# Two MLPs in float32 on one core: w1 in products of 256 columns, its parts laid at other byte offsets per group

## The chip, the core and the metric

One NeuronCore of a Trainium2 chip runs the whole program. The metric is the device time of one execution in microseconds (us). The kernel before takes 2183.7 us, the median of two runs (2183.35 and 2184.06). The execution that was profiled took 2184.25 us. A measurement of this kernel is taken to tell a difference of 2%, which is 43.7 us here.

## The reference, cut to what matters

The model has two layers over 256 tokens of width 2048: stick-breaking attention, an MLP, native sparse attention, and a second MLP. What the change touches is the first half of both MLPs (2048 to 8192 columns) and some projections of the attentions:

```python
def sqrelu_mlp(h, w1, w2):
    return jnp.square(jax.nn.relu(h @ w1)) @ w2

# stick_breaking_attention
q, k, v = jnp.split(h @ w_qkv, 3, axis=-1)
# native_sparse_attention
q, kc, vc, ks, vs, kw, vw, gl = jnp.split(h @ w_in, offs, axis=-1)
```

All arrays are float32, and the result has to be as good as float32. TensorE is used in float32r, which rounds its operands. So each operand is kept as two parts, hi (the rounded value) and lo (what the rounding left), and a product x·w becomes three: xhi·whi, xlo·whi and xhi·wlo.

## The kernel before

The program is one stream of products on TensorE (PE), written out in the order in which it runs. Weights come from HBM in pieces of 512 KB (`load`, L139, on the queue of SP, into five buffers `raw`). ScalarE (ACT) rounds a piece to `hi` (L134), VectorE (DVE) subtracts to get `lo` (L136). `hi` and `lo` have four buffers each.

- **Tile offsets.** `split` (L130) makes its two tiles 64 elements (256 bytes) longer than a piece, and the argument `o` says at which element the piece begins in each: NEAR is 0 bytes, FAR 64 bytes, LOW 208 bytes and SUM 192 bytes. A tile is 4352 bytes long, which is a whole number of 256 bytes, so all four buffers begin at the same remainder modulo 256 bytes. In the built program `xs`, `yhi`, `ylo`, `ss` and the tiles of `hi` and `lo` all begin at that same remainder. So `o`, in bytes, is also the distance modulo 256 between what a product loads as weights and what it streams. This is called the **place** below.
- **proj_T2 (L195)**, used by the first half of the MLPs. `hi` is the stationary operand (the weights in the array), and `xs` holds xhi and xlo side by side, so that one product of 512 columns (L203) makes hi·xhi and hi·xlo at once, into the two halves of one PSUM bank. A second product, of 256 columns (L210), adds lo·xhi to the first half. A piece of 128 by 128 of w1 costs one of each. They run in runs of 16 and 16: two pieces of w1, then the next two. `hi` lies at place 0 and `lo` at place 208.
- **group1 (L440)**. The 8192 columns are done in four groups per MLP (`fg`), each in four blocks of 512 columns (`fb`), so there are 32 blocks in the program. A block has 64 pieces of 128 by 128, and uses four banks of one PSUM pool, `acc` and `att` by turns. At its end ACT copies the second halves (L449, four times), DVE adds the first ones (L450, four times), and one DVE instruction does the relu and the scale by row (L451).
- **proj_T2h (L216)** is the same for 256 columns of weights at a time: four rows of blocks by two, runs of 8 products of 512 columns (L224) and 8 of 256 (L230). It makes q and k of head groups 1 to 3 and the two inputs of the compression: 16 calls of four chunks. `evac_T2` (L237) joins its halves.
- **chunk_T (L178)** serves the first head group alone, at the start of the program. It is the older form: three products of 256 columns for each piece (L185), hi·xhi, hi·xlo and lo·xhi, 16 with `hi` and then 8 with `lo`, both at place 64.
- **The first chunk** is made by `chunk_first` (L547): the same products of 256 columns (L550), with tiles at place 0.
- **group2 (L468)** multiplies by w2. There the weights of the array are `yhi`, `ylo` and `ss`, and w2 streams: products of 512 columns (L156) and, for a quarter of the columns, 21 products of 256 columns per piece (L280, `chunk_S`). w2's parts stream from place 192 there, so that the stationary operand lies 64 bytes past them modulo 256.

Work of the attention and of the next stage is recorded between the products by `pump` (L106), which is called twice per piece.

Of the kernel before, what the change touches and what calls it, by code (L numbers as in the profile page):

```python
# [25 lines left out]
KC = 2  # L26
# [13 lines left out]
def hybrid_kernel(  # L40
# [65 lines left out]
    def pump():  # L106
        if beside:
            b = beside[0]
            b[2] += b[1] / KC
            while b[2] >= 1:  # L110
                b[2] -= 1
                y = next(b[0], b)
                if y is b:
                    beside.remove(b)
                if y:
                    break
# [6 lines left out]

    PAD = 64
    NEAR, FAR, LOW, SUM = 0, 16, 52, 48

    def split(raw, o=(NEAR, NEAR)):  # L130
        n = KC * NB
# [14 lines left out]
    def load_split(*where, o=(NEAR, NEAR)):  # L146
        return split(load(*where), o)

    def bank(pool, tag):
        return pool.tile([P, NB], F32, tag=tag, name=tag)  # L150
# [24 lines left out]
                mm(ahi, lo[:, kk, :], k, t, False, last and kk == KC - 1)  # L175
            pump()

    def chunk_T(ps, src, k0, n0, first, last):  # L178

        hi, lo = src if isinstance(src, tuple) else load_split(src, k0, KC, n0, NB, o=(FAR, FAR))  # L180
        tiles = [(kk, m) for kk in range(KC) for m in range(NB // P)]

        def mm(w, x, kk, m, s, e):
            o = ps[m // 2][:, (m % 2) * T:(m % 2 + 1) * T]
            nc.tensor.matmul(o, w[:, kk, m * P:(m + 1) * P], x[:, k0 + kk, :], start=s, stop=e, skip_group_check=True)  # L185

        for kk, m in tiles:
            mm(hi, xhi, kk, m, first and kk == 0 and m % 2 == 0, False)
            mm(hi, xlo, kk, m, False, False)
        pump()  # L190
        for kk, m in tiles:
            mm(lo, xhi, kk, m, False, last and kk == KC - 1)
        pump()

    def proj_T2(ps, src, n0):  # L195


        for k0 in range(0, KD, 2 * KC):
            parts = [load_split(src, k0 + i * KC, KC, n0, NB, o=(NEAR, LOW)) for i in range(2)]
            tiles = [(k0 + i * KC + kk, m, *(a[:, kk, m * P:(m + 1) * P] for a in parts[i]))  # L200
                     for i in range(2) for kk in range(KC) for m in range(NB // P)]
            for j, (k, m, hi, lo) in enumerate(tiles):
                nc.tensor.matmul(  # L203
                    ps[m], hi, xs[:, k, :, :].rearrange("p a t -> p (a t)"), start=k == 0, stop=k == KD - 1,
                    skip_group_check=True,
                )
                if j % 8 == 7:
                    pump()
            for j, (k, m, hi, lo) in enumerate(tiles):
                nc.tensor.matmul(  # L210
                    ps[m][:, :T], lo, xhi[:, k, :], start=False, stop=k == KD - 1, skip_group_check=True,
                )
                if j % 8 == 7:
                    pump()

    def proj_T2h(src, n0):  # L216

        ps = [bank(acc, "acc") for _ in range(2)]
        KH, W = 2 * KC, NB // 2
        for k0 in range(0, KD, KH):  # L220
            hi, lo = load_split(src, k0, KH, n0, W, o=(NEAR, LOW))
            tiles = [(kk, m) for kk in range(KH) for m in range(2)]
            for kk, m in tiles:
                nc.tensor.matmul(  # L224
                    ps[m], hi[:, kk, m * P:(m + 1) * P], xs[:, k0 + kk, :, :].rearrange("p a t -> p (a t)"),
                    start=k0 + kk == 0, stop=k0 + kk == KD - 1, skip_group_check=True,
                )
            pump()
            for kk, m in tiles:
                nc.tensor.matmul(  # L230
                    ps[m][:, :T], lo[:, kk, m * P:(m + 1) * P], xhi[:, k0 + kk, :],
                    start=False, stop=k0 + kk == KD - 1, skip_group_check=True,
                )
            pump()
        return ps

    def evac_T2(dst, ps, row):  # L237

        c = small.tile([P, 2, T], F32, tag="part", name="part", bufs=1)
        for j in range(2):  # L240
            nc.scalar.activation(c[:, j, :], ps[j][:, T:], AF.Copy)
            nc.vector.tensor_tensor(dst[:, j, :], ps[j][:, :T], c[:, j, :], op=OP.add)
        nc.vector.tensor_tensor(dst, dst, row.unsqueeze(1).to_broadcast([P, 2, T]), op=OP.mult)

    def chunk_S(ps, src, k0, n0, first, last, ahi, alo, shi, slo, koff=0):

# [67 lines left out]
    def proj_N(src, n0, pool=acc, tag="acc"):  # L314
        ps = [bank(pool, tag) for _ in range(NT)]
        for k0 in range(0, KD, KC):
            chunk_N(ps, src, k0, n0, k0 == 0, k0 + KC == KD, xhi, xlo)
        return ps

    def proj_T(src, n0):  # L320
        ps = [bank(acc, "acc") for _ in range(2)]
        for k0 in range(0, KD, KC):
            chunk_T(ps, src, k0, n0, k0 == 0, k0 + KC == KD)
        return ps

    def split_evac(hi, lo, src, scale=None):
# [103 lines left out]
    def mlp(l, layer, junk, done, last=None):  # L430
# [9 lines left out]
        def group1(fg, pools):  # L440

            for fb in range(D // NB):
                ps = [bank(*pools[fb % 2]) for _ in range(NB // P)]
                proj_T2(ps, w1, fg * D + fb * NB)
                k, n = fb * (NB // P), NB // P
                a = junk.tile([P, n, T], F32, tag="pre", name="pre", bufs=1)
                for j in range(n):
                    c = junk.tile([P, T], F32, tag="part", name="part")
                    nc.scalar.activation(c, ps[j][:, T:], AF.Copy)  # L449
                    nc.vector.tensor_tensor(a[:, j, :], ps[j][:, :T], c, op=OP.add)  # L450
                nc.vector.scalar_tensor_tensor(  # L451
                    a, a, 0.0, row.unsqueeze(1).to_broadcast([P, n, T]), op0=OP.max, op1=OP.mult
                )
                s = junk.tile([P, n, T], F32, tag="sq", name="sq", bufs=1)
                nc.scalar.activation(s, a, AF.Square)
                nc.scalar.activation(yhi[:, k:k + n, :], s, AF.Copy)
                nc.vector.tensor_tensor(ylo[:, k:k + n, :], s, yhi[:, k:k + n, :].bitcast(F32), op=OP.subtract)

                sv = s.rearrange("p (j kk) t -> p j kk t", kk=2)
                a1, a2 = [[sv[:, :, kk, t * P:(t + 1) * P] for kk in (1, 0)] for t in range(NT)]  # L460
                q = junk.tile([P, 2, 4, P], F32, tag="sums", name="sums", bufs=1)
                nc.vector.scalar_tensor_tensor(q[:, :, 0, :], a2[0], -1.0, a2[1], op0=OP.mult, op1=OP.subtract)
                nc.vector.tensor_tensor(q[:, :, 2, :], a1[0], a2[0], op=OP.subtract)
                nc.vector.tensor_tensor(q[:, :, 1, :], a2[1], q[:, :, 2, :], op=OP.subtract)
                nc.vector.tensor_tensor(q[:, :, 3, :], a1[1], q[:, :, 1, :], op=OP.subtract)
                split_evac(ss[:, 0, k // 2:k // 2 + 2], ss[:, 1, k // 2:k // 2 + 2], q)
# [44 lines left out]
    with tc.tile_pool(name="sbp", bufs=2) as sp:  # L511
# [171 lines left out]
        for hg in range(NH // HG):  # L683
            qT = sp.tile([P, HG, T], F32, name="qT")
            kT = sp.tile([P, HG, T], F32, name="kT")
            v = sp.tile([P, NT, NB], F32, name="v")
            if hg == 0:
                spawn(first_factors(qT, kT), 1)
            else:
                for b in range(2):  # L690
                    evac_T2(qT[:, 2 * b:2 * b + 2, :], proj_T2h(sb_w_qkv[0], hg * NB + b * T), rows[:, 0, :])
                for b in range(2):
                    evac_T2(kT[:, 2 * b:2 * b + 2, :], proj_T2h(sb_w_qkv[0], D + hg * NB + b * T), rows[:, 1, :])
            psv = proj_N(sb_w_qkv[0], 2 * D + hg * NB, *((att, "att") if hg == 0 else ()))
            for t in range(NT):
                nc.scalar.activation(v[:, t, :], psv[t], AF.Copy, scale=factor[0][:, t:t + 1])

            drain()
            spawn(attention(hg, qT, kT, v), 0.6 if hg < NH // HG - 1 else 1.1)
# [20 lines left out]
    with tc.tile_pool(name="nsa", bufs=2) as ap, ExitStack() as last:  # L720
# [255 lines left out]
        for i in range(2):  # L976
            cT = cp.tile([P, G, T], F32, tag="cT", name="cT", bufs=1)
            for b in range(2):
                ps = proj_T2h(w_in, C0 + i * NB + b * T)
                if rstd is None:  # L980
                    rstd = make_rstd("nsa")
                    pb = bcast_rows(rstd)
                    rb = cp.tile([P, T], F32, name="rb2", bufs=1)
                    nc.scalar.activation(rb, pb[:, :T], AF.Copy)
                evac_T2(cT[:, 2 * b:2 * b + 2, :], ps, rb)
            spawn(compress(i, cT), 1.8)


# [117 lines left out]
```

## Time and profile before

| | |
|---|---|
| median of the runs | 2183.7 us |
| the profiled execution | 2184.25 us |
| its span, first to last instruction | 2182.2 us |
| PE busy | 2172.6 us, 11922 products and as many weight loads |
| DVE busy | 1524.8 us |
| ACT busy | 1210.8 us |
| granted TensorE clock over the span | 1.000 of full speed |

The profile shows a product from its issue to its end, and products overlap. So the time that one product costs is read from the start of one run of products to the start of the next, divided by their number, and not from the duration of one. A row of the view in order of time holds a run of like instructions: its start, the time from the first start to the last end, the engine, line, operation, what it writes and reads, the sizes and the count.

### The profile page before, as it was taken

How to read it: one execution, taken by the hardware profiler on the slowest of the kernel's cores; microseconds unless marked ns; L12 is line 12 of the kernel's file. 1: busy time of each engine (PE TensorE's matmuls, PEld its weight loads, DVE VectorE, ACT ScalarE, POOL GpSimd, SP SyncE). 2: the span in 40 equal slices, each digit the busy share in tenths (PEclk: the TensorE clock that was granted, in tenths of full speed). 3: DMA queues.
4: the chain of work that ended last, by engine and by line, in shares of the span. 5: the costliest groups of instructions: out<-in, count | busy, mean ns of one | idle time of the engine just before them, and what ended most of it. 6: DMA issues, size and time to landing. Idle time of an engine off the chain costs nothing.

```text
span 2182.2 us, 31326 instructions
## 1 busy us (share of the span) xinstructions
PE 2172.6 (100%) x11922; PEld 1880.7 (86%) x11922; DVE 1524.8 (70%) x2096; ACT 1210.8 (55%) x1697; POOL 42.5 (2%) x75
## 2 busy tenths in 40 slices
PE   9999999999999999999999999999999999999999
PEld 9888888888888888888888888888888888888888
DVE  5656656677677677668777877755777676777685
ACT  5555665555455465456555666655554554654553
POOL 0000000000000000000000011000000000000000
PEclk9999999999999999999999999999999999999999
DMA  7655555565665665665667554456656656656664
GB/s 232 206 172 174 157 182 176 181 186 191 205 191 181 216 190 180 217 192 185 206 181 219 160 145 140 137 165 184 188 181 212 193 174 213 193 180 210 191 198 157
DMA packets 260766, 405.97 MB, mean 186 GB/s; under 512 B 13188, under 2 KB 91912, under 8 KB 260616
## 3 DMA queue, kind: packets, MB, share of 16 engines
q1 hardware_dynamic: 259800, 403.52, 59.6%
q8 instruction: 93, 1.52, 0.3%
q10 hardware_dynamic: 816, 0.46, 0.1%
q14 instruction: 57, 0.47, 0.1%
HBM read 401.83 MB, written 2.10 MB: 185 GB/s over the span
## 4 chain that ended last, share of the span: by engine, by line
PE 99%; DVE 0%; POOL 0%; ACT 0%; issue 0%; DVEq 0%; ACTq 0%; POOLq 0%
PE acc L156 31%; PE att L156 13%; PE acc L203 11%; PE att L203 11%; PE acc L210 5%; PE att L210 5%; PE acc L224 5%; PE att L280 4%; PE acc L280 4%; PE acc L230 3%; PE acc L185 2%; PE att L938 1%; PE att L343 1%; PE att L930 0%; PE att L931 0%; PE att L932 0%
## 5 line engine op out<-in xcount | busy, mean ns | idle before, releaser
L136 DVE TENSOR_TENSOR lo<-raw,hi 128x1024 fp32r<-128x1024 f32 x687 | 830.9, 1220 | 386.4 <-issue 170.0
L134 ACT ACTIVATE hi<-raw 128x1024 fp32r<-128x1024 f32 x687 | 726.5, 1059 | 655.7 <-PE acc L156 182.8
L156 PE MATMUL acc<-hi,yhi 128*128 128x512 f32 x640 | 250.7, 392 | 0.0
L156 PE MATMUL acc<-hi,ylo 128*128 128x512 f32 x640 | 249.2, 390 | 0.0
L203 PE MATMUL acc<-xs,hi 128*128 128x512 f32 x1024 | 243.8, 390 | 0.0
L203 PE MATMUL att<-xs,hi 128*128 128x512 f32 x1024 | 243.2, 390 | 0.0
L203 PEld LDWEIGHTS acc<-xs,hi 128*128 128x128 f32 x1024 | 187.8, 188 | 36.2 <-DVE h L399 0.3
L203 PEld LDWEIGHTS att<-xs,hi 128*128 128x128 f32 x1024 | 188.0, 188 | 35.9
L156 PE MATMUL acc<-hi,xs 128*128 128x512 f32 x704 | 177.1, 392 | 0.0
L156 PE MATMUL acc<-lo,yhi 128*128 128x512 f32 x640 | 172.4, 390 | 0.0
L156 PEld LDWEIGHTS acc<-hi,xs 128*128 128x128 f32 x704 | 130.3, 188 | 26.5
L156 PE MATMUL att<-hi,yhi 128*128 128x512 f32 x380 | 148.2, 390 | 0.0
L156 PE MATMUL att<-hi,ylo 128*128 128x512 f32 x380 | 147.9, 389 | 0.0
L156 PEld LDWEIGHTS acc<-lo,yhi 128*128 128x128 f32 x640 | 119.5, 188 | 24.9 <-issue 0.4
L134 ACT ACTIVATE hi<-ts 128x1024 fp32r<-128x1024 f32 x64 | 67.8, 1059 | 130.9 <-DVE ts L260 92.8
L156 PEld LDWEIGHTS acc<-hi,yhi 128*128 128x128 f32 x640 | 120.2, 188 | 23.3 <-ACT yhi L329 0.2
L156 PEld LDWEIGHTS acc<-hi,ylo 128*128 128x128 f32 x640 | 120.2, 188 | 23.2 <-DVE ylo L330 0.2
L210 PEld LDWEIGHTS att<-xs,lo 128*128 128x128 f32 x1024 | 128.4, 188 | 5.2
L254 DVE TENSOR_TENSOR ts<-raw 128x512 f32<-128x512 f32 x64 | 44.2, 691 | 126.3 <-DMA raw<-in_mlp_w_dram 126.3
L210 PEld LDWEIGHTS acc<-xs,lo 128*128 128x128 f32 x1024 | 128.2, 188 | 4.8
L210 PE MATMUL acc<-xs,lo 128*128 128x256 f32 x1024 | 130.1, 278 | 0.0
L210 PE MATMUL att<-xs,lo 128*128 128x256 f32 x1024 | 129.7, 278 | 0.0
(305 smaller groups left out, 3058.1 us busy)
## 6 DMA issues: line engine op xcount, KB each, us to landing
raw<-in_mlp_w_dram SPq DMA_DIRECT2D x512, 512.0 KB, 4.2
raw<-in_sb_w_qkv_dram SPq DMA_DIRECT2D x95, 512.0 KB, 4.0
raw<-in_nsa_w_in_dram SPq DMA_DIRECT2D x50, 512.0 KB, 3.6
raw<-in_sb_w_out_dram SPq DMA_DIRECT2D x32, 512.0 KB, 3.8
raw<-in_nsa_w_in_dram SPq DMA_DIRECT2D x64, 256.0 KB, 3.3
raw<-in_nsa_w_out_dram SPq DMA_DIRECT2D x32, 512.0 KB, 3.8
w1t<-in_nsa_cmp_w_dram SPq DMA_DIRECT2D x8, 512.0 KB, 4.8
h<-in_x_dram SPq DMA_DIRECT2D x8, 256.0 KB, 4.2
```

The source lines that it names most:

```text
L134: nc.scalar.activation(hi, raw, AF.Copy)
L136: nc.vector.tensor_tensor(lo, raw, hi.bitcast(F32), op=OP.subtract)
L156: mm = lambda a, b, k, t, s, e: nc.tensor.matmul(ps[t], a[:, k, t * P:(t + 1) * P], b, start=s, stop=e)
L185: nc.tensor.matmul(o, w[:, kk, m * P:(m + 1) * P], x[:, k0 + kk, :], start=s, stop=e, skip_group_check=True)
L203: nc.tensor.matmul(ps[m], hi, xs[:, k, :, :].rearrange("p a t -> p (a t)"), start=k == 0, stop=k == KD - 1, skip_group_check=True,)
L210: nc.tensor.matmul(ps[m][:, :T], lo, xhi[:, k, :], start=False, stop=k == KD - 1, skip_group_check=True,)
L224: nc.tensor.matmul(ps[m], hi[:, kk, m * P:(m + 1) * P], xs[:, k0 + kk, :, :].rearrange("p a t -> p (a t)"), start=k0 + kk == 0, stop=k0 + ...
L230: nc.tensor.matmul(ps[m][:, :T], lo[:, kk, m * P:(m + 1) * P], xhi[:, k0 + kk, :], start=False, stop=k0 + kk == KD - 1, skip_group_check=True,
L254: nc.vector.tensor_tensor(ts[:, :2, :], flat[:, W:3 * W].rearrange("p (a n) -> p a n", a=2), b12, op=OP.subtract)
L280: nc.tensor.matmul(ps[i], a, w, start=s, stop=e, skip_group_check=True)
L343: nc.tensor.transpose(ps[:, j * T + t * P:j * T + (t + 1) * P], h[:, t, (kp + j) * P:(kp + j + 1) * P], ident)
L938: nc.tensor.transpose(ptp[:w, j * P:(j + 1) * P], src(j), ident)
```

## The change

`proj_T2`, `proj_T2h` and their evacuations go. Both MLPs and the projections use `chunk_T`, which now takes the number of rows of blocks `nk` and the place `o`. The projections (`proj_Th`) lie at FAR, place 64, for both parts. In `group1` the place depends on the MLP, the group and the pair of blocks: with `o = 4 * u` elements, thus 16 * u bytes, u is 1, 2, 3, 5 for the four groups of the first MLP and 7, 9, 11, 13 for those of the second, and 2 more in the last two blocks of each group. Over the 32 blocks that is: place 16 in two, 32 in two, 48 in four, 64 in two, 80 in four, 112 in four, 144 in four, 176 in four, 208 in four and 240 in two.

```diff
-    NEAR, FAR, LOW, SUM = 0, 16, 52, 48
+    NEAR, FAR, SUM = 0, 16, 48
...
-    def chunk_T(ps, src, k0, n0, first, last):
-
-        hi, lo = src if isinstance(src, tuple) else load_split(src, k0, KC, n0, NB, o=(FAR, FAR))
-        tiles = [(kk, m) for kk in range(KC) for m in range(NB // P)]
+    def chunk_T(ps, src, k0, n0, first, last, nk=KC, o=None):
+
+        nm = KC * NB // P // nk
+        hi, lo = src if isinstance(src, tuple) else load_split(src, k0, nk, n0, nm * P, o=o or (FAR, FAR))
+        tiles = [(kk, m) for kk in range(nk) for m in range(nm)]
...
-    def proj_T2(ps, src, n0):
...
+    def proj_T(ps, src, n0, nk=KC, o=None):
+        for k0 in range(0, KD, nk):
+            chunk_T(ps, src, k0, n0, k0 == 0, k0 + nk == KD, nk, o)
+
+    def proj_Th(src, n0):
+
+        ps = bank(acc, "acc")
+        proj_T([ps], src, n0, 2 * KC)
         return ps
...
+    def evac_T(dst, ps, row):
+
+        nc.vector.tensor_tensor(
+            dst, ps.rearrange("p (m t) -> p m t", m=2), row.unsqueeze(1).to_broadcast([P, 2, T]), op=OP.mult
+        )
...
-                ps = [bank(*pools[fb % 2]) for _ in range(NB // P)]
-                proj_T2(ps, w1, fg * D + fb * NB)
+                ps = [bank(*pools[fb % 2]) for _ in range(NB // P // 2)]
+                o = 4 * ((1, 2, 3, 5, 7, 9, 11, 13)[4 * l + fg] + fb // 2 * 2 % 16)
+                proj_T(ps, w1, fg * D + fb * NB, o=(o, o))
...
-                for j in range(n):
-                    c = junk.tile([P, T], F32, tag="part", name="part")
-                    nc.scalar.activation(c, ps[j][:, T:], AF.Copy)
-                    nc.vector.tensor_tensor(a[:, j, :], ps[j][:, :T], c, op=OP.add)
-                nc.vector.scalar_tensor_tensor(
-                    a, a, 0.0, row.unsqueeze(1).to_broadcast([P, n, T]), op0=OP.max, op1=OP.mult
-                )
+                for j in range(0, n, 2):
+                    nc.vector.scalar_tensor_tensor(
+                        a[:, j:j + 2, :], ps[j // 2].rearrange("p (m t) -> p m t", m=2), 0.0,
+                        row.unsqueeze(1).to_broadcast([P, 2, T]), op0=OP.max, op1=OP.mult,
+                    )
```

On PE, at the start of the second block of the first group of the first MLP, before: `xs` is the streamed x, `hi` and `lo` are the parts of w1, `att` is the PSUM pool of the block. These are the first two runs of 16 and 16.

```order
L203 MATMUL att<-xs,hi 128x512 x16
L210 MATMUL att<-xs,lo 128x256 x16
L203 MATMUL att<-xs,hi 128x512 x16
L210 MATMUL att<-xs,lo 128x256 x16
L203 MATMUL att<-xs,hi 128x512 x16
L210 MATMUL att<-xs,lo 128x256 x16
```

The same place now:

```order
L185 MATMUL att<-xs,hi 128x256 x16
L185 MATMUL att<-xs,lo 128x256 x8
L185 MATMUL att<-xs,hi 128x256 x16
L185 MATMUL att<-xs,lo 128x256 x8
L185 MATMUL att<-xs,hi 128x256 x16
L185 MATMUL att<-xs,lo 128x256 x8
```

One pair of rows now covers one piece of w1 (8 blocks of 128 by 128) where a pair before covered two: every product of 512 columns has become two of 256, each with a weight load of its own, and a stretch of products of 512 columns no longer stands between those of 256.

On DVE, at the end of that block, before: `raw`, `hi` and `lo` belong to the next pieces of w1, `part` is what ACT copied, `pre` is the block before the square.

```order
L450 TENSOR_TENSOR pre<-att,part 128x256 x2
L136 TENSOR_TENSOR lo<-raw,hi 128x1024
L450 TENSOR_TENSOR pre<-att,part 128x256 x2
L451 SCALAR_TENSOR_TENSOR pre<-pre,row 128x1024
L136 TENSOR_TENSOR lo<-raw,hi 128x1024
L462 SCALAR_TENSOR_TENSOR sums<-sq 128x2x128
```

The same place now, where L135 makes `lo`, L409 is the relu with the scale, and L421 the first of the sums:

```order
L135 TENSOR_TENSOR lo<-raw,hi 128x1024 x5
L409 SCALAR_TENSOR_TENSOR pre<-att,row 128x512 x2
L135 TENSOR_TENSOR lo<-raw,hi 128x1024
L421 SCALAR_TENSOR_TENSOR sums<-sq 128x2x128
```

Four additions and one long instruction became two, which read PSUM directly, and the four copies on ACT ahead of them are gone. The loads on SP's queue and the instructions on GpSimd stand as they stood.

## Rows read from the trace of the kernel before

**Rows 1.** The page: span and busy time of each engine.
```profile
span 2182.2 us, 31326 instructions
...
PE 2172.6 (100%) x11922; PEld 1880.7 (86%) x11922; DVE 1524.8 (70%) x2096; ACT 1210.8 (55%) x1697; POOL 42.5 (2%) x75
```
**Rows 2.** The page: the chain that ended last, by engine and by line.
```profile
PE 99%; DVE 0%; POOL 0%; ACT 0%; issue 0%; DVEq 0%; ACTq 0%; POOLq 0%
PE acc L156 31%; PE att L156 13%; PE acc L203 11%; PE att L203 11%; PE acc L210 5%; PE att L210 5%; PE acc L224 5%; PE att L280 4%; PE acc L280 4%; PE acc L230 3%; PE acc L185 2%; PE att L938 1%; PE att L343 1%; PE att L930 0%; PE att L931 0%; PE att L932 0%
```
**Rows 3.** Groups by line: line, engine, tiles, count, busy us, mean ns, idle before.
```profile
L203 PE MATMUL acc<-xs,hi 128*128 128x512 f32 x1024 | 243.8, 390 | 0.0
...
L210 PE MATMUL acc<-xs,lo 128*128 128x256 f32 x1024 | 130.1, 278 | 0.0
...
L224 PE MATMUL acc<-xs,hi 128*128 128x512 f32 x512 | 128.2, 392 | 0.0
...
L451 DVE SCALAR_TENSOR_TENSOR pre<-pre,row 128x1024 f32<-128x1024 f32 x32 | 39.1, 1223 | 0.8
...
L399 DVE TENSOR_TENSOR h<-acc,h 128x512 f32<-128x512 f32 x40 | 25.7, 684 | 10.3 <-PE acc L156 10.3
...
L450 DVE TENSOR_TENSOR pre<-att,part 128x256 f32<-128x256 f32 x64 | 23.9, 415 | 0.0
...
L449 ACT ACTIVATE part<-acc 128x256 f32<-128x256 f32 x64 | 22.0, 383 | 13.1 <-DVE pre L450 7.3 <-PE acc L210 5.8
```
**Rows 4.** PE in order of time, second block of the first MLP's first group.
```profile
419.05 3.80 PE L203 MATMUL att<-xs,hi 128*128 128x512 f32 x16
422.69 2.03 PE L210 MATMUL att<-xs,lo 128*128 128x256 f32 x16
424.56 3.80 PE L203 MATMUL att<-xs,hi 128*128 128x512 f32 x16
```
**Rows 5.** PE in order of time, a projection at place 0 and 208.
```profile
102.95 1.99 PE L224 MATMUL acc<-xs,hi 128*128 128x512 f32 x8
104.78 1.09 PE L230 MATMUL acc<-xs,lo 128*128 128x256 f32 x8
105.72 1.99 PE L224 MATMUL acc<-xs,hi 128*128 128x512 f32 x8
```
**Rows 6.** PE in order of time, products of 256 columns at the start.
```profile
9.23 1.12 PE L550 MATMUL acc<-xs,lo 128*128 128x256 f32 x8
10.19 2.05 PE L185 MATMUL acc<-xs,hi 128*128 128x256 f32 x16
12.07 1.11 PE L185 MATMUL acc<-xs,lo 128*128 128x256 f32 x8
13.02 0.60 PE L343 MATMUL att<-ident,h 128*128 128x128 f32 x4
```
**Rows 7.** PE in order of time, chunk_T later in the same stage.
```profile
33.31 1.98 PE L185 MATMUL acc<-xs,hi 128*128 128x256 f32 x16
35.12 1.07 PE L185 MATMUL acc<-xs,lo 128*128 128x256 f32 x8
36.03 0.60 PE L343 MATMUL att<-ident,h 128*128 128x128 f32 x4
```
**Rows 8.** PE in order of time: before, in and after one chunk_S.
```profile
497.83 1.07 PE L156 MATMUL acc<-lo,yhi 128*128 128x512 f32 x4
498.74 0.28 PE L280 MATMUL att<-shi,yhi 128*128 128x256 f32 x1
...
501.21 0.39 PE L156 MATMUL acc<-hi,yhi 128*128 128x512 f32 x1
```
**Rows 9.** Busy us of PE, PEld, DVE, ACT, POOL; PEclk, DMA share, GB/s: one block.
```profile
441.07:463.10 22.03, 22.03 (x130) 19.49 (x129) 15.70 (x20) 12.85 (x16) 0.00 (x0) 1.00 0.63 191
```
**Rows 10.** Groups by line: the splits into hi and lo, idle time and releasers.
```profile
L136 DVE TENSOR_TENSOR lo<-raw,hi 128x1024 fp32r<-128x1024 f32 x687 | 830.9, 1220 | 386.4 <-issue 170.0 <-ACT hi L134 164.4 <-PE att L210 19.4
L134 ACT ACTIVATE hi<-raw 128x1024 fp32r<-128x1024 f32 x687 | 726.5, 1059 | 655.7 <-PE acc L156 182.8 <-PE att L203 146.7 <-PE acc L203 132.0
```

More of the change, by code (lines that the diff above doesn't have):

```diff
@@ L191, in chunk_T @@
         for kk, m in tiles:
-            mm(lo, xhi, kk, m, False, last and kk == KC - 1)
+            mm(lo, xhi, kk, m, False, last and kk == nk - 1)
         pump()
-    def proj_T2(ps, src, n0):
[L198 to L205, printed above, removed]
-                )
[L207 to L234, printed above, removed]
-        return ps
@@ L237, in evac_T2 @@
[L237 to L243, printed above, removed]
+    def proj_T(ps, src, n0, nk=KC, o=None):
+        for k0 in range(0, KD, nk):
+            chunk_T(ps, src, k0, n0, k0 == 0, k0 + nk == KD, nk, o)
@@ L317, in proj_N @@
             chunk_N(ps, src, k0, n0, k0 == 0, k0 + KC == KD, xhi, xlo)
[L318 to L323, printed above, removed]
         return ps
@@ L442, in group1 @@
             for fb in range(D // NB):
-                ps = [bank(*pools[fb % 2]) for _ in range(NB // P)]
-                proj_T2(ps, w1, fg * D + fb * NB)
+                ps = [bank(*pools[fb % 2]) for _ in range(NB // P // 2)]
+                o = 4 * ((1, 2, 3, 5, 7, 9, 11, 13)[4 * l + fg] + fb // 2 * 2 % 16)
+                proj_T(ps, w1, fg * D + fb * NB, o=(o, o))
                 k, n = fb * (NB // P), NB // P
                 a = junk.tile([P, n, T], F32, tag="pre", name="pre", bufs=1)
-                for j in range(n):
-                    c = junk.tile([P, T], F32, tag="part", name="part")
-                    nc.scalar.activation(c, ps[j][:, T:], AF.Copy)
-                    nc.vector.tensor_tensor(a[:, j, :], ps[j][:, :T], c, op=OP.add)
-                nc.vector.scalar_tensor_tensor(
-                    a, a, 0.0, row.unsqueeze(1).to_broadcast([P, n, T]), op0=OP.max, op1=OP.mult
-                )
+                for j in range(0, n, 2):
[3 more added lines that the diff above has]
+                    )
                 s = junk.tile([P, n, T], F32, tag="sq", name="sq", bufs=1)
@@ L690, in hybrid_kernel @@
                 for b in range(2):
-                    evac_T2(qT[:, 2 * b:2 * b + 2, :], proj_T2h(sb_w_qkv[0], hg * NB + b * T), rows[:, 0, :])
+                    evac_T(qT[:, 2 * b:2 * b + 2, :], proj_Th(sb_w_qkv[0], hg * NB + b * T), rows[:, 0, :])
                 for b in range(2):
-                    evac_T2(kT[:, 2 * b:2 * b + 2, :], proj_T2h(sb_w_qkv[0], D + hg * NB + b * T), rows[:, 1, :])
+                    evac_T(kT[:, 2 * b:2 * b + 2, :], proj_Th(sb_w_qkv[0], D + hg * NB + b * T), rows[:, 1, :])
             psv = proj_N(sb_w_qkv[0], 2 * D + hg * NB, *((att, "att") if hg == 0 else ()))
@@ L978, in hybrid_kernel @@
             for b in range(2):
-                ps = proj_T2h(w_in, C0 + i * NB + b * T)
+                ps = proj_Th(w_in, C0 + i * NB + b * T)
                 if rstd is None:
@@ L984, in hybrid_kernel @@
                     nc.scalar.activation(rb, pb[:, :T], AF.Copy)
-                evac_T2(cT[:, 2 * b:2 * b + 2, :], ps, rb)
+                evac_T(cT[:, 2 * b:2 * b + 2, :], ps, rb)
             spawn(compress(i, cT), 1.8)
```

## The prediction, made before the changed kernel ran

> **What bounds the kernel now.** I read the page first. PE is busy for 2172.6 of 2182.2 us [rows 1], and the chain that ended last is PE for 99% of the span, nearly all of it in the lines of products [rows 2]. No other engine sets the end anywhere for long. So the time is the sum of what the products cost on PE, and the question of this change is the price of one product in each form.
>
> I then read PE in order of time, because busy time does not give that price: products overlap. One block of w1 goes in runs of 16 and 16. From the start of one such pair of runs (419.05) to the start of the next (424.56) it is 5.51 us for 16 pieces of 128 by 128 [rows 4]. A block has 64 pieces, thus four pairs of runs: 4 x 5.51 = 22.04 us; the window over one whole block has PE busy for all of its 22.03 us, at granted clock 1.00 [rows 9]. I use 22.03 us for each of the 32 blocks (2048 products of L203 in all, the 1024 of the row and as many into the other pool [rows 3]). By the run of 16 of L203, whose first start to the next run's is 3.64 us, a product of 512 columns costs 227 ns; the run of 16 of L210 takes 1.87 us, so a product of 256 columns at place 208 costs 116.8 ns [rows 4].
>
> Last I looked for products of 256 columns elsewhere, since the changed kernel has nothing else in these stages. They have four prices, all at full clock, and all with the same count of columns and a weight load each:
> - place 0: 8 in 0.96 us, from 9.23 to 10.19: **120.0 ns** [rows 6].
> - place 64, straight behind those: 24 in 2.83 us, from 10.19 to 13.02: **117.9 ns** [rows 6].
> - place 64, later, once the stream has been broken by transposes and waits: 24 in 2.72 us, from 33.31 to 36.03: **113.3 ns** [rows 7].
> - place 208: **116.8 ns** [rows 4].
>
> A fifth reading agrees with the second: in the second half of the MLP 21 products of 256 columns, whose weights also lie 64 bytes past what streams, take 2.47 us from 498.74 to 501.21, thus 117.6 ns each, and they come straight behind products of 512 columns [rows 8]. So the place matters, and at one place there are two rates, of which the stream seems to keep the one that it came in with.
>
> **The change part by part.**
>
> *Blocks of w1.* A piece cost 5.51 / 16 = 344 ns and will cost three products of 256 columns, 192 in a block. The break-even is 22.03 / 192 = 114.7 ns. At 113.3 ns a block takes 21.75 us (0.28 less than before), at 116.8 ns 22.43 (0.40 more), at 117.9 ns 22.64 (0.61 more), at 120.0 ns 23.04 (1.01 more).
> - Four blocks lie at place 208, which has a row: 4 x 0.40 = +1.6 us.
> - Two lie at place 64. They are entered from a running stream of place 32, with no break, so I take 117.9: 2 x 0.61 = +1.2 us (at 113.3 it would be -0.6).
> - The other 26 lie at eight places that no row shows. The bounds are the nearest rows, the cheapest and the dearest price of this form: 113.3 (26 x -0.28 = -7.3 us) and 120.0 (26 x 1.01 = +26.3 us). Between them I take the mean of the four prices, (120.0 + 117.9 + 113.3 + 116.8) / 4 = 117.0 ns, since nothing tells me to which place an unknown one is nearest: 192 x 117.0 = 22.46 us, 0.43 more, 26 x 0.43 = +11.3 us. Most entries into these blocks are from products of 512 columns without a pause, as in rows 8, which speaks for the upper half rather than the lower.
>
> *The projections.* A chunk of 8 pieces took 2.77 us, from 102.95 to 105.72 [rows 5]. There are 64 of them (512 products of L224 [rows 3], 8 to a chunk). Now a chunk is 24 products at place 64: 2.72 us at 113.3, 2.83 at 117.9. That is -3.2 or +3.8 us for all. Attention's products stand between these chunks and bring the stream into either rate, so I take the middle, +0.3 us.
>
> *Evacuation.* A block loses four copies on ACT (383 ns) and four additions (415 ns) and one instruction of 1223 ns on DVE, and gets two on DVE that read 512 columns of PSUM, for which the nearest row is 684 ns [rows 3]: DVE 4 x 415 + 1223 - 2 x 684 = 1.5 us less, ACT 1.5 us less. None of it is on PE's path: in a block DVE is busy for 15.70 us and ACT for 12.85 of 22.03 [rows 9], and PE doesn't stop between blocks. The gain is 0. What it costs if the cover is gone: nothing is added on these engines, so no cover is used up. Two banks in place of four are held per block, so a block can only get its banks sooner.
>
> *The splits and loads.* As many pieces are loaded and split as before. ACT's split waits for PE to free a buffer (its largest releasers are products [rows 10]), so the buffers are full ahead of PE, and a piece that is used up over 24 x 117 ns = 2.8 us is needed no faster than before (5.51 / 2). I count 0. If the cover went, the price would be the split's own 1.06 us on ACT and 1.22 on DVE per piece [rows 10], which fit into 2.8 us side by side. The places only shift where the two write, and no row shows them minding it.
>
> *The sum.* 1.6 + 1.2 + 11.3 + 0.3 = +14.4 us on the profiled execution: 2184.25 + 14.4 = 2198.7. That execution lies 0.55 us above the median of the runs (2183.7), so I forecast **2198 us**, +0.7%.
>
> A rule speaks against this. The Trainium skill (TensorE: Matmul & The Clock Gate, Step-by-step: what each phase is for) says that TensorE has two independent read ports into SBUF, and that loading the next weights takes no read bandwidth from the running product. By that the place could not matter, and all products of 256 columns would run at the rate of rows 7. The trace disagrees: rows 4 and 6 have three dearer prices for the same work. I keep the rows; the rule's outcome is the first rival below.
>
> **The rivals.**
>
> *1. The place hardly matters, and a long stream finds the low rate.* The dearer prices come from short runs: 8, 24, 16 and 21 products. A block has 192 in a row, and rows 7 show that the stream can reach 113.3 ns. Then the 32 blocks give 32 x -0.28 = -9.0 us and the projections -3.2, so 2171.5 us: faster than before, by 0.6%. It decides once the mean over all blocks falls below 114.7 ns. Against it: in rows 6 the rate held over all 24 products at place 64 without falling.
>
> *2. The unknown places are at the dear end.* If they cost what place 0 does, and place 64 keeps its dear rate in the projections too: +26.3 + 1.6 + 1.2 + 3.8 = +32.9 us, 2216.5 us. For it: three of the four prices lie above the break-even, and the one below it was reached behind pauses only. Against it: 208, only 48 bytes off 0 modulo 256, already costs 3.2 ns less than place 0.
>
> *3. A place at which a weight load isn't covered at all.* For more than 2% (43.7 us) the 26 blocks would have to give 43.7 - 1.6 - 1.2 - 3.8 = 37.1 us, 1.43 each, thus 23.46 / 192 = 122.2 ns on average. No run of such products in the rows is that dear, but eight places are unseen.
>
> **How the numbers follow.** The likeliest, a mixture of rates that averages 115.5 to 119 ns, I give 0.64; its own range is 2185 to 2212. Rival 1 and what lies near it get 0.15, rival 2 0.16, rival 3 0.04; 0.01 is left for a gain of over 2%, which no row offers. A range of 2175 to 2216 leaves about 0.1 out below and 0.1 above. Within 2% is 0.95, since even the two bounds, 2171.5 and 2216.5, lie within it.
>
> **What would show it.** In the changed kernel, read PE in order of time over each pair of blocks: 192 products of L185 per block, and the start-to-start time of blocks gives the price at each place. Right: different times at different places, between 21.75 and 23.04 us, place 208 at 22.4. Wrong: the same 21.75 at all places (rival 1), most at 23.0 (rival 2), or gaps on PE that a split or a bank ends, which none of my terms holds. ACT's copies and DVE's additions should be gone, without any effect on the end.

## The result, and the profile after

The changed kernel takes **2204.43 us** (median of two runs, 2204.0 and 2204.85), the kernel before 2183.7. The ratio is 1.0092, with a 95% interval of 1.0068 to 1.0116: 0.9% slower, within 2%. The profiled execution took 2204.0 us with a span of 2202.3, so 20.1 us more than before [rows 1].

The page of the changed kernel, its first lines (span and busy time) and the engines of the chain that ended last:

```profile
span 2202.3 us, 36040 instructions
...
PE 2192.2 (100%) x14482; PEld 2003.3 (91%) x14482; DVE 1484.3 (67%) x1968; ACT 1163.8 (53%) x1537; POOL 42.6 (2%) x75
...
PE 99%; DVE 0%; DMA 0%; POOL 0%; ACT 0%; issue 0%; SPq 0%; DVEq 0%; ACTq 0%
```

PE is still the whole chain, with 2560 products more. DVE lost 40.5 us of busy time and ACT 47.0, as the edit of the evacuation said, and each of the two has 0% of the chain that ended last.

The groups by line of the changed kernel (line, engine, tiles, count, busy us, mean ns, idle before): the products with `hi`, and the one instruction that evacuates now, beside its three forerunners of [rows 3]:

```profile
L185 PE MATMUL acc<-xs,hi 128*128 128x256 f32 x3312 | 422.4, 280 | 2.1 <-ACT hi L133 2.1
...
L185 PE MATMUL att<-xs,hi 128*128 128x256 f32 x2048 | 263.1, 281 | 0.0
...
L409 DVE SCALAR_TENSOR_TENSOR pre<-acc,row 128x512 f32<-128x512 f32 x32 | 20.6, 685 | 16.8 <-PE acc L185 16.8
```

The splits (L133) are the only thing that PE waits for in these lines, 2.1 us in the whole program. In the kernel before L185 waited for them too, 1.9 us:

```profile
L185 PE MATMUL acc<-xs,hi 128*128 128x256 f32 x240 | 30.4, 279 | 1.9 <-ACT hi L134 1.9
```

So the 20 us are in the price of a product. PE in order of time shows it: the starts of blocks at places 48 (entered from place 16), 64, 112 and 208, and what follows them (start, us, engine, line, tiles, sizes, count).

```profile
441.57 2.05 PE L185 MATMUL acc<-xs,hi 128*128 128x256 f32 x16
...
464.18 2.04 PE L185 MATMUL att<-xs,hi 128*128 128x256 f32 x16
...
617.34 1.98 PE L185 MATMUL att<-xs,hi 128*128 128x256 f32 x16
...
639.10 1.98 PE L185 MATMUL acc<-xs,hi 128*128 128x256 f32 x16
...
660.86 0.40 PE L155 MATMUL att<-hi,yhi 128*128 128x512 f32 x1
...
967.67 2.08 PE L185 MATMUL att<-xs,hi 128*128 128x256 f32 x16
...
990.71 2.08 PE L185 MATMUL acc<-xs,hi 128*128 128x256 f32 x16
...
1013.74 0.40 PE L155 MATMUL att<-hi,yhi 128*128 128x512 f32 x1
...
1892.24 2.03 PE L185 MATMUL acc<-xs,hi 128*128 128x256 f32 x16
...
1914.64 2.03 PE L185 MATMUL att<-xs,hi 128*128 128x256 f32 x16
```

A block is 192 products whatever its place, but 464.18 - 441.57 = 22.61 us at place 48, 21.76 at 64, 23.04 at 112 and 22.40 at 208. Read in this way, all places of the changed kernel (without the first block of each MLP, where other work stands between the products):

| place | us per block | ns per product |
|---|---|---|
| 64 | 21.76 | 113.3 |
| 208 | 22.40 | 116.7 |
| 48 | 22.61 behind place 16, 22.72 behind products of 512 columns | 117.8, 118.3 |
| 176 | 22.67 | 118.1 |
| 16, 32 | 22.72 | 118.3 |
| 80 | 22.8 | 118.8 |
| 112, 144, 240 | 23.04 | 120.0 |

Places 80, 112, 144, 176 and 208 were entered in two ways, from another place and from products of 512 columns or from transposes; their two prices differ by 0.2 ns at most. The block before took 22.03 us [rows 9]. The start-to-start sums over the program: the 32 blocks 727.5 us against 705.7 (+21.8), the projections 176.5 against 178.0 (-1.45), the rest of the stream 1250.6 against 1251.0 (-0.35), the wait for the first data +0.2.

Busy time by engine (PE, PEld, DVE, ACT, POOL; granted clock, DMA share, GB/s) for two blocks at place 48 and two at 64 in the changed kernel:

```profile
441.57:486.79 45.22, 45.22 (x386) 45.22 (x385) 31.16 (x36) 23.66 (x24) 0.00 (x0) 1.00 0.62 186
617.34:660.86 43.52, 43.52 (x387) 43.52 (x385) 30.80 (x35) 23.65 (x24) 0.00 (x0) 1.00 0.64 193
```

Both run at the full granted clock (2.4 GHz), with PE without a gap, with the same number of weight loads and 8.4 MB moved in each. PEld, which had 2.5 us free per block before [rows 9], is now busy all the time. What differs between the two rows is where the weights lie, and the place from which the stream came in.

### The profile page after: what moved, and what is told of

Its sections match the earlier page's. It is cut to its first block, busy times and chain, and to the rows that moved or that the text cites. A ratio compares the mean times of both kernels' runs of the same rounds, so it can differ in the third digit from the quotient of the medians.

```text
span 2202.3 us, 36040 instructions
## 1 busy us (share of the span) xinstructions
PE 2192.2 (100%) x14482; PEld 2003.3 (91%) x14482; DVE 1484.3 (67%) x1968; ACT 1163.8 (53%) x1537; POOL 42.6 (2%) x75
## 4 chain that ended last, share of the span: by engine, by line
PE 99%; DVE 0%; DMA 0%; POOL 0%; ACT 0%; issue 0%; SPq 0%; DVEq 0%; ACTq 0%
PE acc L155 31%; PE acc L185 26%; PE att L185 17%; PE att L155 13%; PE att L246 4%; PE acc L246 4%; PE att L897 1%; PE att L303 0%; PE att L889 0%; PE att L890 0%; PE att L891 0%; PE att L584 0%; PE att L632 0%; PE att L843 0%; DMA raw<-in_sb_w_qkv_dram 0%; PE att L845 0%
## 5 line engine op out<-in xcount | busy, mean ns | idle before, releaser
L133 ACT ACTIVATE hi<-raw 128x1024 fp32r<-128x1024 f32 x687 | 726.1, 1059 | 749.0 <-PE acc L155 218.8
L135 DVE TENSOR_TENSOR lo<-raw,hi 128x1024 fp32r<-128x1024 f32 x687 | 836.2, 1221 | 401.3 <-ACT hi L133 385.1
L185 PE MATMUL acc<-xs,hi 128*128 128x256 f32 x3312 | 422.4, 280 | 2.1 <-ACT hi L133 2.1
L185 PEld LDWEIGHTS acc<-xs,hi 128*128 128x128 f32 x3312 | 401.9, 188 | 3.1 <-ACT hi L133 2.5
L185 PE MATMUL att<-xs,hi 128*128 128x256 f32 x2048 | 263.1, 281 | 0.0
L185 PEld LDWEIGHTS att<-xs,hi 128*128 128x128 f32 x2048 | 251.5, 188 | 0.3
L185 PE MATMUL acc<-xs,lo 128*128 128x256 f32 x1656 | 227.4, 280 | 0.0
L185 PEld LDWEIGHTS acc<-xs,lo 128*128 128x128 f32 x1656 | 208.0, 188 | 0.0
L155 PEld LDWEIGHTS acc<-lo,yhi 128*128 128x128 f32 x640 | 119.5, 188 | 24.9 <-issue 0.4
L185 PE MATMUL att<-xs,lo 128*128 128x256 f32 x1024 | 142.0, 281 | 0.0
L185 PEld LDWEIGHTS att<-xs,lo 128*128 128x128 f32 x1024 | 130.1, 188 | 0.0
L133 ACT ACTIVATE hi<-ts 128x1024 fp32r<-128x1024 f32 x64 | 67.8, 1060 | 94.3 <-DVE ts L226 45.8
```

The source lines that it names most:

```text
L133: nc.scalar.activation(hi, raw, AF.Copy)
L135: nc.vector.tensor_tensor(lo, raw, hi.bitcast(F32), op=OP.subtract)
L155: mm = lambda a, b, k, t, s, e: nc.tensor.matmul(ps[t], a[:, k, t * P:(t + 1) * P], b, start=s, stop=e)
```

## The experiments

None of them changes what is computed. Edits are to the changed kernel unless said otherwise; `o` counts elements of 4 bytes. The kernel before was timed again beside each set of runs, and the ratios are to those times: a median of 2187.4 us for the first two ratios below, 2185.1 for the next two and 2185.2 for the last three. My theory was that the place, together with the way in which the stream came in, sets the price; the main rival was that long runs find the low rate by themselves.

**All of w1 at place 64.**

```diff
-                proj_T(ps, w1, fg * D + fb * NB, o=(o, o))
+                proj_T(ps, w1, fg * D + fb * NB)
```

> All 32 blocks of w1 lie at place 64. Theory (the price of a product of 256 columns is set by its place, and at place 64 by the state in which the stream comes in: straight from products of 512 columns it stays at 117.8 ns): the six groups that follow group2 without a pause stay at 117.8, 22.6 us in each of their 24 blocks, and the two groups that begin among transposes fall to 113.3, 21.8 us in the blocks behind the first. Against before that is 24 x 0.59 - 8 x 0.27 and 1.4 less in the projections, thus about +10 us, 2194. Rival (the dear state lasts only for short runs, and a block of 192 finds 113.3 by itself): 21.8 us in all blocks, 32 x -0.27 - 1.4 = -10 us, about 2173.5.

Measured: 2196.36 us, ratio to before 1.0045 (1.0029 to 1.0062). PE in order of time, in the first group of the first MLP and over the start of the second:

```profile
418.53 1.98 PE L185 MATMUL att<-xs,hi 128*128 128x256 f32 x16
...
440.29 1.98 PE L185 MATMUL acc<-xs,hi 128*128 128x256 f32 x16
...
567.99 1.07 PE L155 MATMUL acc<-lo,yhi 128*128 128x512 f32 x4
568.90 2.05 PE L185 MATMUL att<-xs,hi 128*128 128x256 f32 x16
...
591.51 2.05 PE L185 MATMUL acc<-xs,hi 128*128 128x256 f32 x16
...
614.13 2.05 PE L185 MATMUL att<-xs,hi 128*128 128x256 f32 x16
```

The same place has two rates. The groups that begin among transposes run at 21.76 us per block (113.3 ns); the six that begin straight behind products of 512 columns run at 22.61 (117.8 ns), through all four blocks, thus 768 products. A long run doesn't find the low rate: it keeps the one it came in with.

**The same, with the first 24 products of each group at place 32.** If the entry decides, another entry should turn all groups cheap.

```diff
+            chunk_T(ps, src, k0, n0, k0 == 0, k0 + nk == KD, nk, o0 if o0 and k0 == 0 else o)
...
+                proj_T(ps, w1, fg * D + fb * NB, o0=(8, 8) if fb == 0 else None)
```

> As all places at 64, but the first 24 products of each group lie at place 32. In the changed kernel two blocks at place 64 that came straight from place 32 ran at 113.3 ns. Theory (the state of entry decides): the 24 products cost 118.3 and all behind them 113.3, so every block takes about 21.8 us and the time is about 2174, some 20 us less than with place 64 from the start. Rival (short runs alone are dear): no difference from the run with place 64 throughout. Second rival (the two cheap blocks were cheap for another reason, such as their group): the groups stay at 117.8, about 2194.

Measured: 2178.45 us, ratio 0.9963 (0.995 to 0.9976). The start of the second group:

```profile
568.21 2.06 PE L185 MATMUL att<-xs,hi 128*128 128x256 f32 x16
570.10 1.11 PE L185 MATMUL att<-xs,lo 128*128 128x256 f32 x8
571.05 1.98 PE L185 MATMUL att<-xs,hi 128*128 128x256 f32 x16
...
590.09 1.98 PE L185 MATMUL acc<-xs,hi 128*128 128x256 f32 x16
...
611.85 1.98 PE L185 MATMUL att<-xs,hi 128*128 128x256 f32 x16
```

24 products at 118.3 ns, and then the rest of the group at 113.3: a block of 21.76 us where it was 22.61. The time is 17.9 us less than with place 64 throughout, where some 20 were expected. 24 products of 192 in one block of four turned a kernel slower than before into a faster one.

**More places.** Sixteen in one kernel, two blocks each, then sixteen pairs of blocks in a second kernel by what those gave, nine of its places new.

```diff
-                o = 4 * ((1, 2, 3, 5, 7, 9, 11, 13)[4 * l + fg] + fb // 2 * 2 % 16)
+                o = ((0, 24), (32, 40), (48, 56), (10, 12), (13, 14), (15, 17), (18, 19), (20, 22))[4 * l + fg][fb // 2]
```

> Two blocks each at places 0, 96, 128, 160, 192, 224, 40, 48, 52, 56, 60, 64, 68, 72, 76, 80 and 88 (one pair at each but what the groups give). Theory (only a narrow stretch around place 64 is cheap): 113.3 ns at 64 and perhaps at 60 to 68, and 116.5 to 120 at all others, with 120 at 0 and 128. Rival (the price repeats every 128 bytes, as 16 bytes past 128 costs what 16 before 128 does): 192 is as cheap as 64, and 128 is like 0.

Measured: 2203.05 us in one run. For the second scan the pairs were (22, 21), (22, 23), (13, 11), (19, 9), (25, 26), (25, 27), (28, 7), (22, 5).

> Steps of 4 bytes around the cheap places of the scan (52, 64, 76, 88 at 113.3, twelve bytes apart, 56, 60, 68, 72, 80 at 117.8 to 119.5). Entered straight from products of 512 columns: 88, 52, 76, 100, 28, and 64 not at all. Theory (the cheap places recur every 12 bytes, and how they are entered decides): 100 and 28 or 40 can be cheap, 84, 92, 44, 36, 104, 108, 20 are not; of the cheap ones some stay at 117.8 when entered from 512 columns, as 64 does. Rival (88 and 76 are the only ones that lock by themselves, as they lie further on): 88 and 76 are at 113.3 from the first block, 52 isn't.

Measured: 2204.95 us in one run. From the starts of blocks in both (the expectation of the first scan names place 64, which stands there in the projections alone):

| ns per product | places |
|---|---|
| 113.3 | 88 (from 512 columns and from place 80), 76 (from 512 columns and from 72), 52 (behind transposes) |
| 116.7 | 20, 28, 224 |
| 117.3 to 117.8 | 96, 56, 192, 44, 104 |
| 118.3 to 119.5 | 48, 68, 72, 92, 80, 40, 60 |
| 120.0 | 0, 36, 84, 100, 108, 112, 128, 160; 52 from 512 columns |

Place 52 shows both rates. The block starts, first in the first scan (52, then 56), then in the second (52 twice, 76 twice):

```profile
1519.88 1.98 PE L185 MATMUL att<-xs,hi 128*128 128x256 f32 x16
...
1541.64 2.05 PE L185 MATMUL acc<-xs,hi 128*128 128x256 f32 x16
```

```profile
748.38 2.08 PE L185 MATMUL acc<-xs,hi 128*128 128x256 f32 x16
...
771.42 2.08 PE L185 MATMUL att<-xs,hi 128*128 128x256 f32 x16
...
924.75 1.99 PE L185 MATMUL att<-xs,hi 128*128 128x256 f32 x16
...
946.53 1.98 PE L185 MATMUL acc<-xs,hi 128*128 128x256 f32 x16
```

With 64, the cheap places found are 52, 64, 76 and 88, 12 bytes apart. So the first theory, that only a narrow stretch around 64 is cheap, is wrong: 60 and 68 are dear. The rival that the price repeats every 128 bytes falls too: in the changed kernel 80 and 208, both straight behind products of 512 columns, cost 118.7 and 116.7 ns, and 32 costs 118.3 where 160 costs 120.0. (The 117.8 ns of 192 would not decide it, as that is also the higher rate of 64 behind 512 columns.) My guess that the steps of 12 bytes go on falls as well, by the entries tried: 40, 28 and 100 are dear. What the rival of the second scan said came out, 88 and 76 cheap from the first block behind 512 columns and 52 not; its reason, that they lie further on, is not shown.

**Is it the address of the weights, or the distance to what streams?** `xs` moved 32 bytes on; w1 at 64 in the first MLP (distance 32) and at 96 in the second (distance 64). A second filler behind `xs` fills up the 256 bytes, so that what lies further on keeps its remainder.

```diff
+    cpool.tile([P, 8], F32, name="before_xs")
...
+    cpool.tile([P, 56], F32, name="after_xs")
...
+                o = (16, 24)[l]
```

> xs begins 32 bytes further on, while w1 keeps its places: 64 past the old remainder in the first MLP, 96 in the second. Theory (the distance between what is loaded and what streams decides): the first MLP runs at the price of place 32, 118.3 ns, 22.7 us a block, and the second is at distance 64, 113.3 or 117.8 by its entry. Rival (the weights' own address decides): the first MLP at 113.3 or 117.8, the second at whatever place 96 costs in the scan.

Measured: 2208.48 us in one run. Starts of blocks in the first MLP, then in the second (`chunk_T` is L187 there):

```profile
449.75 2.06 PE L187 MATMUL acc<-xs,hi 128*128 128x256 f32 x16
...
472.47 2.06 PE L187 MATMUL att<-xs,hi 128*128 128x256 f32 x16
...
1703.51 1.98 PE L187 MATMUL acc<-xs,hi 128*128 128x256 f32 x16
...
1725.27 1.98 PE L187 MATMUL att<-xs,hi 128*128 128x256 f32 x16
```

Address 64 at distance 32 takes 22.72 us, the price of place 32. Address 96, which cost 117.3 in the scan, takes 21.76 at distance 64. So the distance decides which prices a place has, and not the address. Which of its two rates place 64 took is another matter: here the group behind transposes stayed at 117.8 ns and those behind 512 columns were cheap, the reverse of the run with all of w1 at 64.

**hi and lo at different places.** Pairs of (64, 208, 0, 32), to see which product pays for which.

```diff
+                o = (((16, 16), (16, 52)), ((16, 0), (52, 16)), ((0, 16), (0, 52)), ((52, 0), (8, 16)),
+                     ((16, 16), (16, 52)), ((16, 0), (52, 16)), ((0, 16), (0, 52)), ((52, 0), (8, 16)))[4 * l + fg][fb // 2]
```

> hi and lo of a piece lie at different places: (64, 64), (64, 208), (64, 0), (208, 64), (0, 64), (0, 208), (208, 0), (32, 64), two blocks each in both MLPs. Theory (each product pays for its own place, by distance): (64, 208) is 128 x 113.3 + 64 x 116.7 = 22.0 us a block, (0, 208) 128 x 120 + 64 x 116.7 = 22.8, (208, 0) 128 x 116.7 + 64 x 120 = 22.6, and (0, 64) either 22.6 or 22.9, as its lo enters from place 0, behind which place 64 ran at 117.9 at the start of the program. Rival (the price belongs to the tile of hi alone, or to how the two lie to each other): (64, 208) equals (64, 64), or (0, 208) equals (208, 0).

Measured: 2196.69 us in one run. One block with hi at 64 and lo at 208, and one with hi at 208 and lo at 0:

```profile
463.32 1.98 PE L185 MATMUL att<-xs,hi 128*128 128x256 f32 x16
465.14 1.09 PE L185 MATMUL att<-xs,lo 128*128 128x256 f32 x8
...
2037.82 2.03 PE L185 MATMUL acc<-xs,hi 128*128 128x256 f32 x16
2039.69 1.11 PE L185 MATMUL acc<-xs,lo 128*128 128x256 f32 x8
```

In the first the sixteen take 1.82 us (113.8 ns), in the second 1.87 (116.9). Each run of products pays mostly for its own place: (64, 208) took 21.97 us per block, (0, 208) 22.78, (208, 0) 22.55, near the weighted means of the single prices. Both rivals fall: (64, 208) is dearer than (64, 64), which took 21.76, and (0, 208) differs from (208, 0). (64, 0) took 22.72, more than 113.3 for the sixteen would give: each run at 64 that follows one at 0 stays near 117.8 ns, as in [rows 6].

**All of w1 at place 88**, which like 76 was cheap both behind products of 512 columns and behind another place.

```diff
+                proj_T(ps, w1, fg * D + fb * NB, o=(22, 22))
```

> All blocks of w1 at place 88. In the scan 88 was at 113.3 when it came straight from place 80. If it takes the cheap rate from any entry: 21.8 us in all 32 blocks, about 2176, as with the first 24 products at place 32. If it needs an entry of its own like place 64: 22.6 us in the 24 blocks behind group2, about 2196.

Measured: **2175.59 us, ratio 0.9953 (0.9938 to 0.9968)**. Page and the start of the second group:

```profile
span 2173.5 us, 36040 instructions
...
PE 2163.5 (100%) x14482; PEld 1974.1 (91%) x14482; DVE 1482.8 (68%) x1968; ACT 1162.9 (54%) x1537; POOL 42.5 (2%) x75
```

```profile
568.34 2.00 PE L185 MATMUL att<-xs,hi 128*128 128x256 f32 x16
570.17 1.07 PE L185 MATMUL att<-xs,lo 128*128 128x256 f32 x8
...
590.12 1.98 PE L185 MATMUL acc<-xs,hi 128*128 128x256 f32 x16
...
611.88 1.98 PE L185 MATMUL att<-xs,hi 128*128 128x256 f32 x16
```

The first four products behind 512 columns cost 117 to 121 ns, the rest of the blocks 113.3, at 21.76 to 21.78 us per block in all groups. With the same instructions as the changed kernel this is 28.8 us of span less. It has the lowest median of all kernels here and is faster than the kernel before and the changed one; its interval and that of the kernel with place 32 at the entry overlap, so those two are not told apart.

**The kernel before, with its run of 256 columns at 88.**

```diff
-    NEAR, FAR, LOW, SUM = 0, 16, 52, 48
+    NEAR, FAR, LOW, SUM = 0, 16, 22, 48
```

> The kernel before with one number changed: lo at place 88 in place of 208, so that runs of 16 products of 256 columns come straight from runs of 512 columns. Theory (distance and entry decide in that kernel too): if place 88 takes the cheap rate from 512 columns, a run of 16 costs 1.81 us and not 1.87, 160 runs of 16 in all (2048 + 512 products), and the time falls by 2560 x 3.4 = 8.7 us, to about 2175. If it doesn't, the runs are at 117.8 and the time rises by 2.8 us.

Measured: 2182.59 us, ratio 0.999 (0.998 to 1.0). A pair of runs:

```profile
600.63 2.00 PE L210 MATMUL acc<-xs,lo 128*128 128x256 f32 x16
602.46 3.81 PE L203 MATMUL acc<-xs,hi 128*128 128x512 f32 x16
606.11 2.00 PE L210 MATMUL acc<-xs,lo 128*128 128x256 f32 x16
```

The sixteen went from 1.87 to 1.83 us, but the run of 512 columns behind them from 3.64 to 3.65: 5.48 to 5.49 us per pair against 5.51 [rows 4]. A run of 16 at 113.3 ns would have saved 0.06 us per pair; the first four products cost 474 ns and not 453, and the first five of 512 columns behind them 1160 ns, where they cost 1144 in the kernel before. So the two changes of form take more than half of the gain, and neither of the two outcomes I had written down came.

**More at 88: the projections, then also the sums of group2, then all at 76.**

```diff
-    NEAR, FAR, SUM = 0, 16, 48
+    NEAR, FAR, SUM = 0, 22, 48
```

with w1 at 88 as well (the projections); `SUM = 42` beside it for the sums; 19 and 45, with w1 at 19, for place 76.

> As all blocks at place 88, and the projections and the first stage too (their 1536 products were at 113.3 or 117.8 by their entry). Theory (88 takes the cheap rate from any entry within some 5 products): the stretches that stayed at 117.8 fall to 113.3, some 2 us less than with the blocks alone at 88, about 2173.5. Rival (entries behind attention's small products leave 88 dear as well): no change.

> As e9, and the parts of w2 in the runs of 21 products lie at place 168, so that the stationary operand lies 88 bytes past them, not 64. There the roles are exchanged: w2 streams. Theory (the distance alone decides, whoever streams): the runs fall from 117.7 to 113.3 behind their first four products, 64 runs x 17 x 4.4 ns = 4.8 us less than e9, if the entry is cheap, and at least 2 us. Rival (the weights' own address decides, which isn't moved here): no change to e9.

> As e10 with 76 bytes in place of 88 for all three. In the scan 76 took the cheap rate from products of 512 columns, as 88 does: within 2 us of e10.

Measured: the projections 2178.36 us, ratio 0.9971 (0.9959 to 0.9982); with the sums 2182.06, ratio 0.9983 (0.9974 to 0.9993); place 76 2186.58, ratio 1.0007 (0.9997 to 1.0016). All three miss. The median with the projections is 2.8 us above that with the blocks alone at 88, where 2 less were expected; with the sums it is another 3.7 higher, where the theory had a gain and the rival no change; and place 76 lies 4.5 us behind place 88, where 2 were allowed. (In the first two steps the intervals overlap; the causes below are read from the traces.) A projection at 88, in order of time:

```profile
1124.33 2.03 PE L185 MATMUL acc<-xs,hi 128*128 128x256 f32 x16
1126.20 1.10 PE L185 MATMUL acc<-xs,lo 128*128 128x256 f32 x8
1127.13 2.03 PE L185 MATMUL acc<-xs,hi 128*128 128x256 f32 x16
```

24 products in 2.80 us, 116.7 ns: 88 has a second rate too. Here the stream came into it behind two products of 128 columns (L352), and in the head groups behind attention's products of q and k (120 products in 14.08 us); behind products of 512 columns the projections took the low rate. In all they took 177.8 us against 176.5 at place 64, so the rival's reason was right in part. In the profiled execution 1.6 us more were lost at the start, where the granted clock was 0.83 between 10 and 20 us, thus 1.2 GHz for some of it and 2.4 for the rest. In the sums, one chunk of 21 products:

```profile
500.69 0.28 PE L246 MATMUL att<-shi,yhi 128*128 128x256 f32 x1
...
503.21 0.39 PE L155 MATMUL acc<-hi,yhi 128*128 128x512 f32 x1
```

2.52 / 21 = 120.0 ns, where it was 117.6 [rows 8]. There what is loaded and what streams have exchanged their roles, and 88 is a dear distance: the theory that the distance alone decides, whoever streams, is wrong. The nine products of 512 columns behind such a chunk got dearer too, 232 ns each in the mean where they were 227. Together that is 0.09 us for each of the 64 chunks, 5.8 us in the profiled execution. At 76 the groups behind 512 columns were cheap, but one that begins among transposes is locked at the other rate:

```profile
421.90 2.08 PE L185 MATMUL att<-xs,hi 128*128 128x256 f32 x16
...
444.94 2.08 PE L185 MATMUL acc<-xs,hi 128*128 128x256 f32 x16
```

23.04 us per block, 120.0 ns, where place 64 in the same group had 21.76.

## Why the prediction was right

It said 2198 us and a range of 2175 to 2216; the kernel takes 2204.4, above the forecast and inside the range. The mechanism was right: PE is the whole chain, the price goes by place, every block lies between 21.76 and 23.04 us, and place 208 takes 22.40. By its own steps:

- **The break-even of 114.7 ns** held. Every block above it lost, the two below it gained, and the kernel with all blocks at 113.3 is faster than before.
- **Four blocks at place 208, +1.6 us**: they took 22.40 us each, +1.5. Right.
- **Two blocks at place 64, +1.2**: they took 21.76 each, -0.5. Wrong, in the choice of 117.9 for a stream that enters without a break. The first two experiments show why: from place 32 the stream enters the low rate, from 512 columns it entered the high one.
- **26 blocks at unseen places, +11.3**: they gave +20.8, by the sums over blocks (21.8 - 1.5 + 0.5). This is the mis-sized term, in the words "I take the mean of the four prices, 117.0 ns": the mean was 22.83 / 192 = 118.9 ns. One of the four prices, 113.3, is that of a state found at few places (4 of some 30 that were run), so a plain mean of four gave it far too much weight. My own remark that the entries speak for the upper half pointed the right way, but its reason is not what the runs show: at the unseen places that were entered in two ways the entry moved the price by 0.5 ns at most. They are dear by their place.
- **The projections, +0.3**: -1.45. The middle was wrong: most of them run at 113.3, entered from attention's products. Straight behind 512 columns they were seen at the high rate.
- **Evacuation and splits, 0**: right. DVE and ACT lost 40.5 and 47.0 us of busy time, PE has no gap in the blocks, and its wait for the splits grew by 0.2 us, from 1.9 to 2.1.

With measured sizes the sum is 1.5 - 0.5 + 20.8 - 1.45 = +20.3, where the span shows +20.1; the rest of the stream and the start make up -0.15. The largest term was 9.5 us too small and two others together 3.5 us too large, so that the forecast missed by 6 us and not by 9.5 is luck.

Rival 1, that long streams find the low rate, is out: 768 products in a row stayed at 117.8 ns. The Trainium skill (TensorE: Matmul & The Clock Gate, Step-by-step: what each phase is for) has the weights read by a port of their own that takes nothing from the running product. The traces disagree with what the prediction drew from it, that the place could not matter: at one clock, with the same loads, a product costs 113.3 ns at place 64 and 120.0 at 112, and moving `xs` alone moved the price. Whether the two reads share bandwidth, no run here shows. Rival 2 was near in size for the unseen places (118.9 where it had 120.0), and wrong on the projections, most of which were cheap. Rival 3, a place beyond 120 ns, did not occur in the changed kernel's blocks: 120.0 is the dearest price at any place.

**What stays open.** The runs show that the distance modulo 256 and the entry set the price (the buffers lie 4352 bytes, 17 times 256, apart, and all pieces of a block cost the same), not what in the chip does it: why the cheap places are 12 bytes apart, and why one place has two lasting rates. Which entry leads where is known case by case only; it turned round between two kernels at distance 64. Not tried: another entry for the projections at 88 and for the sums of group2, other entries for most of the dear places of the scans, and products of 512 columns at other places.

## What to carry to other kernels

The price of a product of 256 columns with a weight load of its own can hang on the distance in bytes between the two operands: read it from start to start over long runs, at each place, before trading one product of 512 columns and one of 256 for three of 256. Choose a place that is cheap from every entry that it will have, or put a few products at another place ahead, and measure it in the program itself: a price from elsewhere in the kernel didn't carry over three times here. A mean over observed prices is a poor guess for unseen cases when the cheapest of them was reached in special circumstances only.

## What the runs showed that I had not expected

- A stream of equal products has two lasting rates at one place: 113.3 and 117.8 ns at 64, 113.3 and 116.7 at 88, 113.3 and 120.0 at 52 and at 76.
- 24 products at place 32 ahead of a group move the next 744 from 117.8 to 113.3 ns.
- The low rate, 113.3 ns, is half of a product of 512 columns (227 ns [rows 4]), so in this state the three products cost 340 ns where the pair before, 512 columns and 256 at place 208, cost 344.
